# Low parts of eight weight blocks in an encoder's mixer made by an accumulating DMA instead of VectorE

## The chip, the cores and the metric

The kernel runs on one core of one Trainium2 chip. The metric is device time in microseconds (us) of one execution; before the change it is 876.37 us, the median of 3 runs (875.76 to 877.21). Engines are named as in the profile: PE is TensorE (its matmuls; PEld its weight loads), DVE is VectorE, ACT is ScalarE, POOL is GpSimd, SP is SyncE, which issues most DMAs.

## The reference

One encoder layer on 512 positions of 1024 channels: a half-step SwiGLU, a mixer and a second half-step SwiGLU, each behind an RMSNorm, and a final norm. The change is in the mixer:

```python
h = rms_norm(x, mix_norm)
u = h @ w_in                       # 512 Fourier columns | 8 query heads | 2 key heads | 2 value heads
f_out = fourier_mixer(u[..., :o0], fnet_w, fnet_b)     # real part of a 2-D DFT per group, then a 128x128 map per group
a_out = gqa_attention(u[..., o0:o1], u[..., o1:o2], u[..., o2:], q_norm, k_norm)
x = x + jnp.concatenate([f_out, a_out], axis=-1) @ w_out
```

Queries and keys are normed per head and rotated by position; the attention is a plain softmax over all 512 positions.

## The kernel before

**Products in three passes.** All data is float32. A factor is split into a high part, rounded to the type fp32r that PE takes, and a low part, the exact difference. `product` (L108) makes three matmuls: high by high (L109), high by low (L110) and low by high (L111). So each 128x1024 block of weights (`weights`, L95) needs three steps before PE can use it: a load from DRAM into one of three raw buffers (`raw_tile`, L85, on SP's queue), a rounded copy to the high part (L101 on ACT; L99 on DVE for the names in `HI_DVE`, the first two Fourier blocks), and a subtraction on DVE for the low part (`lows`, L72). The third pass alone reads the weights' low part.

**A second way** exists for a few blocks of the first FFN, `rest_by_dma` (L90): ACT writes minus the high part into the low part's place (L92), and a DMA issued by POOL reads the weights from DRAM once more and adds them there (L93). In the kernel before, the four gate blocks with `by_dma` and two activation tiles (L270) take it.

**Slots.** High and low parts live in slots of 128x1024: four of `ring` and two more that the mixer adds (`more`, L610), handed out in turn by `slot` (L77). So three blocks of weights are there at a time, and a block's copy waits until PE has done the block three before it.

**The mixer (L608 to L983).** It multiplies the normed activations by the key block (`in0`), the first query block (`in1`), the values (`in5`) and three further query blocks (`in2` to `in4`), then by four Fourier blocks (`f0` to `f3`, `fload` and `fproject`) and, through `fold`, by the map's weights `fw`, which have half the size. Keys, queries and values pass through `rope`, `query`, `keys` and `value_stacks`, which are work for ACT and DVE. Three tables for the Fourier part (`chan`, `pos`, `odd`, L903) are loaded by POOL at the start.

**Attention and filling.** For 32 pairs of a query tile and a 128-row group, `scores` makes two matmuls on PE, a maximum on DVE (L842) and an exponential on ACT (L845); `turn` transposes the probabilities on PE (L851), copies them rounded on ACT (L854) and subtracts on DVE; `values` makes two matmuls with them (L870, L871). Between these steps the list `fill` spreads the remaining products: query blocks 1 to 3, the eight pieces of the Fourier projection, the fold and the DFT. Each entry has a cost, and entries are taken in order until their sum keeps up with the share of attention steps done (L965 to L972). The blocks' loads are entries of cost 0 in this list (`load`, `fload`).

**What sets the order.** In the FFNs PE and SP keep the order in which the program is written (`in_order`, L64). The mixer stands outside of that: there the order of the instructions on every engine is settled when the program is built, by a model of their times and with earlier lines of the program going first among those that are ready. On the chip each engine then runs its own list strictly in order.

Of the kernel before, what the change touches and what calls it, by code (L numbers as in the profile page):

```python
# [31 lines left out]
PIECES = (0, 2, 2, 1, 1, 1, 1)  # L32
KH = KD // 2
HI_DVE = ("f0", "f1")
SWAP_DMA = ("q1", "q2", "q3")


def asf(ap):
    return ap.bitcast(F32)
# [3 lines left out]
def encoder(ctx, tc, A, out):  # L43
# [27 lines left out]
    def lows(lo, src, hi):  # L71
        nc.vector.tensor_tensor(out=lo, in0=src, in1=asf(hi), op=ALU.subtract)  # L72
# [9 lines left out]
    def weight_slots():  # L82
        return (slot().rearrange("p (a b) -> p a b", b=P) for _ in range(2))

    def raw_tile(src, name, n=KD):  # L85
        raw = wp.tile([P, KD, P], F32, tag="raw", name=f"raw_{name}")
        nc.sync.dma_start(out=raw[:, :n, :], in_=src)
        return raw

    def rest_by_dma(lo, hi, src):  # L90

        nc.scalar.activation(lo, asf(hi), AF.Copy, scale=-1.0)  # L92
        nc.gpsimd.dma_start(out=lo, in_=src, accum_op=ALU.add)  # L93

    def weights(src, name, n=KD, raw=None, by_dma=False):  # L95
        raw = raw or raw_tile(src, name, n)
        hi, lo = weight_slots()
        if name in HI_DVE:
            nc.vector.tensor_copy(hi[:, :n, :], raw[:, :n, :])  # L99
        else:  # L100
            nc.scalar.copy(hi[:, :n, :], raw[:, :n, :])  # L101
        if by_dma:
            rest_by_dma(lo, hi, src)
        else:
            lows(lo[:, :n, :], raw[:, :n, :], hi[:, :n, :])
        return hi, lo
# [6 lines left out]
    class Norm:  # L113
# [36 lines left out]
        def add(self, k):  # L150
            self.scale(k)
            self.sums(k)
# [55 lines left out]
    def ffn(norm, after, wgu, wd, wdt, opening, closing):  # L208
# [6 lines left out]
        with tc.tile_pool(name=f"act{n_}", bufs=1) as ap, tc.tile_pool(name=f"sums{n_}", bufs=2) as sp:  # L215
# [11 lines left out]
            def gate(c, between={}, by_dma=False):  # L227
                whi, wlo = weights(wgu[c], f"gu{n_}_{c}", by_dma=by_dma)
                ps = bank(f"gu{n_}_{c}")
                for k in range(KD):  # L230
                    between.get(k, int)()
                    product(ps, whi[:, k, :], wlo[:, k, :], hh[k], hl[k], k == 0, k == KD - 1)
                return ps
# [169 lines left out]
            def down(d, group, gi):  # L403

                js = [j for j in group if j != "t"]
                whi, wlo = weights(wd[d][:, js[0] : js[-1] + 1, :], f"dn{n_}_{d}_{gi}", len(js))
                w = wt[d // 4][:, d % 4 * P : (d % 4 + 1) * P]

                def steps(ps, t):
                    for i, j in enumerate(group):  # L410
                        h, l = (at[:, where[j], o, t] for o in range(2))
                        first, last = i == 0, i == len(group) - 1
                        if j == "t":
                            nc.tensor.matmul(ps[:, t], w, h, start=first, stop=False)
                            nc.tensor.matmul(ps[:, t], w, l, start=False, stop=last)
                        else:
                            k = j - js[0]
                            product(ps[:, t], whi[:, k, :], wlo[:, k, :], h, l, first, last)
                        yield

                return steps
# [186 lines left out]
    with tc.tile_pool(name="mix", bufs=1) as mp, tc.tile_pool(name="mixt", bufs=1) as mt:  # L608
# [18 lines left out]
        def project(c, name):  # L627

            whi, wlo = weights(A["wins"][c], f"in{c}")
            ps = bank(name)  # L630
            banks[name] = ps

            def step(k):
                product(ps, whi[:, k, :], wlo[:, k, :], hh[k], hl[k], k == 0, k == KD - 1)

            return [(0.65, step, (k,)) for k in range(KD)]
# [3 lines left out]
        def rope(name, g):  # L640
# [4 lines left out]
            sw = tp.tile([P, S], F32, tag="g", name=f"sw_{name}")  # L645
            if name in SWAP_DMA:
                own = mt.tile([P, S], F32, tag="own", name=f"own_{name}")
                nc.scalar.activation(own, ps, AF.Copy, scale=g)
            for b in range(4):
                o, i = b * 32, (b ^ 1) * 32  # L650
                if name in SWAP_DMA:
                    nc.sync.dma_start(out=sw[o : o + 32], in_=own[i : i + 32])
                else:
                    nc.scalar.activation(sw[o : o + 32], ps[i : i + 32], AF.Copy, scale=g[i : i + 32])
            r = tp.tile([P, S], F32, tag="u", name=f"rot_{name}")
            if name in SWAP_DMA:
                nc.vector.tensor_tensor(out=r, in0=own, in1=cos, op=ALU.mult)
# [266 lines left out]
        for t in (1, 2, 3):  # L924
            for k in range(KD):
                add(step, t, k, cost=0.65)
                if k == 0 and t < 3:
                    add(load, t + 1)
                if t == 3 and k in (0, 4):
                    add(fload, k // 4)  # L930
                if k == 3:
                    add(*((value_stacks,) if t == 1 else (heads, f"q{t - 1}", t, scale)), cost=0.3)
            add(query, t)
# [235 lines left out]
```

## Time and profile before

The profiled execution took 877.47 us, 875.7 of them the span of the program, with a mean granted clock of 0.996. From the page and the trace:

| what | value |
|---|---|
| median of runs | 876.37 us (875.76 to 877.21) |
| profiled execution, span | 877.47 us, 875.7 us |
| first matmul of the key block | 351.58 us |
| first matmul of the values, and the first that reads their low part | 364.67 and 365.22 us |
| first matmul of the Fourier blocks | 402.38 us |
| first matmul of the fold | 454.91 us |
| subtraction for a 128x1024 low part (L72, DVE) | 1.22 us |
| rounded copy of 128x1024 (L101, ACT) | 1.05 us |
| such a copy on DVE (L99) | 0.69 us |
| plain load of 512 KB, from issue to landing | 3.4 to 3.8 us at the median, by group |

Busy time says how long an engine had instructions running. A wait is idle time of an engine, put down to the instruction that ended last among those it waited for. What a wait of PE costs is time; what another engine waits for costs nothing unless PE waits for it in turn.

### The profile page before, as it was taken

Reading aid. Unit: us, or ns where it says so; the run is one execution under the profiler, and the core shown is the slowest. Engines: PE = TensorE matmul, PEld = TensorE weight load, DVE = VectorE, ACT = ScalarE, POOL = GpSimd, SP = SyncE. Lnnn points to the kernel's source line nnn. Section 1 sums busy time; section 2 is a strip of 40 time slices with the busy share of each in tenths; the row PEclk is TensorE's granted clock in tenths of the full one; section 3 lists DMA queues with packets and bytes.
Section 4 is the critical chain, followed back from the end, with each engine's and each line's share of the span. In section 5 each row is a group of like instructions: output and inputs, shape, how many; then the busy total and the mean of one; then the engine's idle time right before and its main releaser. Section 6 shows DMA issues by size and latency. Waiting matters only on the chain.

```text
span 875.7 us, 13587 instructions
## 1 busy us (share of the span) xinstructions
PE 862.0 (98%) x5391; PEld 769.1 (88%) x5391; DVE 640.8 (73%) x1011; ACT 459.0 (52%) x763; POOL 27.8 (3%) x33
## 2 busy tenths in 40 slices
PE   8999999999999999999999999999999999999996
PEld 6788998899989998888888888889998999889986
DVE  7798985488746837699888558987974698559554
ACT  7663664266524644677776445535652366226541
POOL 0110000000000000211000000000000000000001
PEclk9999999999999999999999999999999999999999
DMA  7664322323243113621110224242323232323212
GB/s 263 154 150 149 133 85 73 115 97 120 78 140 108 49 51 109 205 79 43 49 49 25 77 70 142 85 133 97 109 79 127 75 117 99 97 101 104 73 37 97
DMA packets 30609, 88.46 MB, mean 101 GB/s; under 512 B 3665, under 2 KB 8529, under 8 KB 30417
## 3 DMA queue, kind: packets, MB, share of 16 engines
q1 hardware_dynamic: 28304, 82.87, 28.3%
q0 software_dynamic: 1696, 4.20, 2.4%
q8 instruction: 42, 0.69, 0.3%
q10 hardware_dynamic: 544, 0.52, 0.2%
q14 instruction: 23, 0.18, 0.1%
HBM read 83.91 MB, written 2.10 MB: 98 GB/s over the span
## 4 chain that ended last, share of the span: by engine, by line
PE 94%; ACT 2%; DVE 2%; DMA 1%; issue 1%; SPq 0%; POOL 0%; DVEq 0%; ACTq 0%
PE r L338 22%; PE q L338 11%; PE dn L109 8%; PE dn L111 8%; PE dn L110 8%; PE p L338 6%; PE gu L109 3%; PE gu L111 3%; PE gu L110 3%; PE out L109 2%; PE out L111 2%; PE out L110 2%; PE pt L851 1%; PE q L109 1%; PE q L110 1%; PE q L111 1%
## 5 line engine op out<-in xcount | busy, mean ns | idle before, releaser
L338 PE MATMUL r<-rt,ring 128*128 128x256 f32 x1632 | 213.0, 282 | 0.0
L338 PEld LDWEIGHTS r<-rt,ring 128*128 128x128 f32 x1632 | 201.8, 188 | 2.4
L109 PE MATMUL dn<-at,ring 128*128 128x512 f32 x303 | 119.7, 395 | 0.0
L110 PE MATMUL dn<-at,ring 128*128 128x512 f32 x303 | 119.6, 395 | 0.0
L111 PE MATMUL dn<-at,ring 128*128 128x512 f32 x303 | 119.6, 395 | 0.0
L338 PE MATMUL q<-rt,ring 128*128 128x256 f32 x816 | 107.9, 281 | 0.0
L424 DVE SCALAR_TENSOR_TENSOR gx<-dn,gx 128x512 f32<-128x512 f32 x61 | 42.1, 690 | 82.0 <-PE dn L111 82.0
L338 PEld LDWEIGHTS q<-rt,ring 128*128 128x128 f32 x816 | 101.6, 188 | 0.0
L72 DVE TENSOR_TENSOR ring<-s,ring 128x1024 fp32r<-128x1024 f32 x68 | 82.9, 1221 | 17.8 <-PE r L338 10.9
L101 ACT CAST ring<-raw_dn 128x768 fp32r<-128x768 f32 (+1 forms) x59 | 45.5, 775 | 92.9 <-PE dn L110 78.8
L299 ACT CAST ring<-s 128x1024 fp32r<-128x1024 f32 x68 | 71.4, 1050 | 38.1 <-PE r L338 18.4
L111 PEld LDWEIGHTS dn<-at,ring 128*128 128x128 f32 x303 | 56.9, 188 | 13.8 <-DVE ring L72 0.2
L110 PEld LDWEIGHTS dn<-at,ring 128*128 128x128 f32 x303 | 57.0, 188 | 13.1
L109 PEld LDWEIGHTS dn<-at,ring 128*128 128x128 f32 x303 | 56.9, 188 | 13.0
L72 DVE TENSOR_TENSOR ring<-raw_dn,ring 128x768 fp32r<-128x768 f32 (+1 forms) x59 | 51.8, 881 | 7.2 <-ACT ring L101 6.2
L72 DVE TENSOR_TENSOR ring<-raw_g,ring 128x1024 fp32r<-128x1024 f32 x34 | 41.6, 1224 | 17.7 <-PE p L338 10.7
L338 PE MATMUL p<-rt,ring 128*128 128x256 f32 x408 | 54.0, 281 | 0.0
L338 PEld LDWEIGHTS p<-rt,ring 128*128 128x128 f32 x408 | 50.8, 188 | 0.0
L299 ACT CAST ring<-raw_g 128x1024 fp32r<-128x1024 f32 x34 | 35.7, 1049 | 22.2 <-DMA raw_g<-in_wgu 9.0
L308 ACT CAST ring<-raw_u 128x512 fp32r<-128x512 f32 x34 | 21.1, 621 | 39.3 <-PE dn L111 19.9
L383 DVE TENSOR_TENSOR u<-g,u 128x512 f32<-128x512 f32 x34 | 23.4, 688 | 15.9 <-ACT u L382 15.9
L109 PE MATMUL gu<-ring 128*128 128x512 f32 x80 | 31.3, 392 | 0.0
(328 smaller groups left out, 1579.9 us busy)
## 6 DMA issues: line engine op xcount, KB each, us to landing
raw_dn<-in_wd SPq DMA_DIRECT2D x48, 384.0 KB, 3.1
raw_g<-in_wgu SPq DMA_DIRECT2D x34, 512.0 KB, 3.8
raw_u<-in_wgu SPq DMA_DIRECT2D x34, 512.0 KB, 4.4
raw_gu<-in_wgu SPq DMA_DIRECT2D x14, 512.0 KB, 3.5
raw_o<-in_wo SPq DMA_DIRECT2D x8, 512.0 KB, 3.6
raw_dn<-in_wd SPq DMA_DIRECT2D x16, 192.0 KB, 2.4
raw_in<-in_wins SPq DMA_DIRECT2D x6, 512.0 KB, 3.6
raw_f<-in_winf SPq DMA_DIRECT2D x4, 512.0 KB, 3.8
```

The source lines that it names most:

```text
L72: nc.vector.tensor_tensor(out=lo, in0=src, in1=asf(hi), op=ALU.subtract)
L101: nc.scalar.copy(hi[:, :n, :], raw[:, :n, :])
L109: nc.tensor.matmul(ps, whi, mhi, start=first, stop=False)
L110: nc.tensor.matmul(ps, whi, mlo, start=False, stop=False)
L111: nc.tensor.matmul(ps, wlo, mhi, start=False, stop=last)
L299: nc.scalar.copy(hi, src)
L308: nc.scalar.copy(hi, src)
L338: nc.tensor.matmul(ps, a[:, ks], b[:, i], start=first and i == 0 and o == 0, stop=i == KH - 1 and o == 2, skip_group_check=not first,)
L383: nc.vector.tensor_tensor(out=u, in0=b["g"], in1=u, op=ALU.mult)
L424: nc.vector.scalar_tensor_tensor(out=x[d][:, t], in0=ps[:, t], scalar=0.5, in1=x[d][:, t], op0=ALU.mult, op1=ALU.add)
L851: nc.tensor.transpose(pt[:, c * P : (c + 1) * P], prob[t, b, c][:, kc * P : (kc + 1) * P], ident)
```

## The change

The names in a new list, `LOW_DMA`, take the second way in `weights`: the values (`in5`), query blocks 1 to 3 (`in2` to `in4`), Fourier blocks 0 to 2 and the map's weights. The key block, the first query block and the last Fourier block keep the subtraction on DVE. `rest_by_dma` gets slices, since the map's weights fill half a tile. And the entry that starts Fourier block 1 in the list `fill` stands behind step 1 of the last query block, not behind step 4.

```diff
 HI_DVE = ("f0", "f1")
+LOW_DMA = ("in5", "in2", "in3", "in4", "f0", "f1", "f2", "fw")
 SWAP_DMA = ("q1", "q2", "q3")
...
-        if by_dma:
-            rest_by_dma(lo, hi, src)
+        if by_dma or name in LOW_DMA:
+            rest_by_dma(lo[:, :n, :], hi[:, :n, :], src)
         else:
             lows(lo[:, :n, :], raw[:, :n, :], hi[:, :n, :])
...
-                if t == 3 and k in (0, 4):
-                    add(fload, k // 4)
+                if t == 3 and k in (0, 1):
+                    add(fload, k)
```

## The prediction

> **What bounds the kernel now.** I read the engine totals first, then the list of what TensorE (PE) waited for in the mixer, then busy times by stage, and last the order of work round each stall. The totals:
>
> ```profile
> PE 862.0 (98%) x5391; PEld 769.1 (88%) x5391; DVE 640.8 (73%) x1011; ACT 459.0 (52%) x763; POOL 27.8 (3%) x33
> ```
>
> PE is busy for 862.0 of 875.7 us: at most 13.7 us can be had from waits, wherever they are. The change touches only the mixer, whose first load is used at 351.58 us and whose last probabilities are used near 478. There PE waited for this (us in total, times, longest):
>
> ```profile
> PE o L870 <- ACT ph L854: 1.4, 2, 0.9
> PE f L761 <- ACT e L845: 1.2, 1, 1.2
> PE s L838 <- ACT e L845: 0.5, 1, 0.5
> PE pt L851 <- ACT e L845: 0.4, 1, 0.4
> ```
>
> The sum is 3.5 us, and that is the ceiling of any gain (0.4%). By the order of time the five stalls are 1.25 us up to 402.38, 0.90 up to 435.83, 0.49 up to 457.03, 0.40 up to 464.71 and 0.48 up to 469.46. The stages, with the columns PE, PEld, DVE, ACT, POOL, granted clock, DMA share, GB/s:
>
> ```profile
> 345.00:370.00 25.00, 25.00 (x120) 20.77 (x120) 16.01 (x25) 14.96 (x21) 5.30 (x5) 1.00 0.53 179
> 370.00:385.00 15.00, 15.00 (x79) 12.57 (x78) 14.45 (x31) 10.08 (x18) 1.64 (x1) 1.00 0.26 83
> 385.00:400.00 15.00, 15.00 (x83) 12.47 (x82) 14.50 (x30) 11.88 (x26) 1.64 (x1) 1.00 0.24 58
> 400.00:415.00 15.00, 13.75 (x99) 12.42 (x98) 13.39 (x33) 11.49 (x24) 3.89 (x3) 1.00 0.11 36
> ...
> 430.00:445.00 15.00, 14.10 (x100) 12.74 (x99) 12.07 (x26) 9.32 (x21) 0.87 (x1) 1.00 0.12 38
> ```
>
> From 370 to 400 VectorE (DVE) is busy 28.95 of 30 us and ScalarE (ACT) 21.96. PE hides that until 401. So DVE is the fuller helper, but every stall of PE ends on an ACT instruction.
>
> **What each sum by DMA costs.** The first FFN already makes low parts this way, and those rows are the price list (ns: min, median, max; the first for the extra copy, the second for the issue and, in us, from issue to landing):
>
> ```profile
> L92 ACT ACTIVATE ring<-ring x3: 1056/1057/1064, 26.3 to 45.0; 128x1024 fp32r<-128x1024 f32 x3
> ```
>
> ```profile
> L93 POOL DMA_DIRECT2D ring<-in_wgu x3: 854/875/1109, 27.6 to 46.3; - x3
> ...
> DMA to landing us min/median/max: 5.2/5.7/7.5
> ```
>
> Removed from DVE: seven subtractions of 128x1024 at 1.22 us (L72, from raw_in and raw_f) and one of 128x512 at 0.68 (raw_fw): 7 x 1.22 + 0.68 = 9.2 us. Added to ACT: seven copies of minus the high part at 1.06 and one of half the size, which I estimate at 0.63 from the 512-wide copies: 8.0 us. Added to GpSimd (POOL): eight issues of some 0.9 us, 7.2 us in all. The low part is then there about 1.06 + 5.7 = 6.8 us after the high part, not 1.2. The weights are also read a second time: in the stretch 20 to 60 us six such sums (2.88 MB) took 42.8% of 40 us of all 16 engines, 3.1 us for each 512 KB, while 3.90 MB of plain loads took 28.8%, 1.5 us for 512 KB.
>
> **Which low part comes late.** For each block I compare the high part's end with the first matmul that needs the low part. Queries: high parts end at 358.1, 365.3 and 371.4. Their extra copies may stand behind the rope and key copies on ACT (free again at 361.4, 369.4, 375.1), so sums are issued by about 362.5, 370.4 and 376.2 and land by 369.5, 376.5 and 382.5; needed at 372.1, 378.3 and 387.8. Fourier blocks: needed from 402.6 (cast 378.1), 404 (cast 386.4) and 428 (cast 394.2), the map's weights (cast 426.0) at 454.9. All these are in time by 2 us or more and cost PE nothing; if the cover of the third block in the list (needed at 378.3) were gone, each us of lateness is a us of PE.
>
> The values' block is the tight one. Its high part runs 352.49 to 353.54, the squares of the closing FFN follow on ACT until 354.7, so I put the extra copy at 354.7 to 355.75 and the issue at 355.8. By then three tables stand ahead of it on POOL's queue:
>
> ```profile
> pos<-in_pos POOLq DMA_DIRECT2D x1, 1028.0 KB, 9.4
> ...
> chan<-in_chan POOLq DMA_DIRECT2D x1, 256.0 KB, 3.9
> ...
> odd<-in_odd POOLq DMA_DIRECT2D x1, 1.0 KB, 9.2
> ```
>
> odd has 1 KB, was issued at 353.17 and took 9.2 us: it came behind pos, so this queue goes in order. pos lands at 352.63 + 9.4 = 362.0. The DMA engines are full (share 0.97 to 1.01 from 358 to 362, 0.28 by 363 to 364). If the sum's data starts at 361 it takes 3.1 us alone and up to 2 more beside what is left of the loads, and some 1 us to be seen: 365 to 367. PE needs it at 365.22, the third matmul of the values. **Cost +1.0 us** (bounds 0 and +2.5). Behind that matmul on PE stand the key transposes, the head sums and the next query block; nothing else can go ahead of them there. Before it, v's first two matmuls run as now.
>
> The Trainium skill's page "DMA: Bandwidth & Descriptors", section "Anatomy of one DMA — SWDGE (gpsimd) path", gives 2.0 us plus bytes over 436 GB/s, an estimate of 3.2 us for 512 KB. The trace has 5.2 to 7.5 us for the accumulating form, so I use the trace; by the page's figure the sum would start with pos gone and be there by about 364, and the total below would be 1.0 us lower. The same page, section "Queues, rings and completion order", says that a ring's descriptors are consumed in order while an engine goes round between the rings, with which odd's 9.2 us agrees.
>
> **What the freed DVE time is worth.** The stall at 402.38 ends with an exponential that ACT starts at 401.43. ACT had run without a gap from 394.18 to 398.94 (the cast of the third Fourier block, then the last query's square, its scaled copy and its casts, a probability cast, an exponential), and then waited for PE's transposes. So there ACT, not DVE, is in front: the third Fourier block's extra 1.06 us may fall just there. On the other hand the exponentials waited 11.2 us in eleven places for DVE's maxima, and DVE loses 4 x 1.22 = 4.9 us of work between 372 and 397. Bounds: the whole stall gone (-1.25), or two extra copies (second and third Fourier block) in front of it (+2.1). I take -0.4, since ACT still has idle time to take the copies, 3.1 us in 384 to 401. The stall at 435.83 goes back to DVE, full from 424.2 to 432.6, with an exponential that waited 3.0 us for it: one subtraction of 0.68 fewer there, and ACT idle to take the map's copy. I take -0.6 (bounds -0.9 and 0). The last three stalls lie among the output weights' casts, which stay as they are: 0, between -1.4 (the order of the engines outside the FFNs is set anew when the program is built) and +1.0 by the same token.
>
> **The moved load.** Three things of that block can move. Its load is already out at 366.61 on SP, right behind the first block's, held by a raw buffer and not by its place; on SP nothing of this stage stands between. Its cast on DVE starts at 386.36, 0.2 us after the second query's last matmul frees the slots (386.16 to 386.55), and a place three steps earlier can't pass that. Its sum is issued at about 388.2 on POOL, ahead of or behind one power of 1.64 us for the heads, and is needed at 404. Cost 0; if the power had to wait for the issue, 0.9 us that the 8 us to the scales' use cover. Raw buffers come free 1.2 us sooner, which only moves loads that wait for nothing.
>
> **Sum.** +1.0 - 0.4 - 0.6 + 0 = 0.0 us on the profiled execution, 877.47 us (875.7 of span and 1.8 around it). It lies 1.1 us above the median of the runs, 876.37, so I forecast 876.4 for the median. About 0.2%, or 1.75 us, is what a measurement can tell from no change.
>
> **Rivals.** (1) DVE is what holds the attention stage back. For it: 28.95 of 30 us busy, and the exponentials' 11.2 us. Against it: every stall ends on ACT, and 402.38's is full of ACT work. Then the first two stalls go (-2.15), and if the new order clears part of the last three (1.37) and the values' sum is in time, -2.2 to -3.5: about 873.5.
>
> (2) ACT takes DVE's place, which makes it slower. Place: 384 to 401, where ACT has 3.1 us idle in pieces of about 0.9 and gets two extra copies of 1.06; a piece too short moves every exponential behind it. Each moved exponential holds its bank and so the scores and the Fourier matmuls. Price 2.1 us there and some 0.5 among the keys (ACT full from 370.3 to 375.1): +2.5, so 878.9. It decides once ACT's idle time in that stretch is under 1 us. Against it: most waits of the exponentials end on DVE.
>
> (3) The values' sum lands at 368, because the copy and its issue come late or the loads of the queries crowd it: PE stands 2.5 to 3 us at 365.22, nothing is won back, 879. For it: full DMA engines and an in-order queue. Against it: by 363 these engines are nearly idle.
>
> **How the numbers follow.** Forecast 0.34, with its own range 874.8 to 878.0; rival 1 0.32; rival 2 0.20; rival 3 0.14. Faster than 874.6: 0.28 of rival 1 and 0.03 of the forecast, 0.31. Slower than 878.1: 0.16 of rival 2, 0.12 of rival 3 and 0.03 of the forecast, 0.31. The rest, 0.38, is within 0.2%. The range 873.2 to 879.6 takes in rivals 1 and 2 and most of 3, and leaves about a tenth on each side.
>
> **What would show it.** The values' third matmul (L111, out v) with an idle time before it, released by a DMA, shows the first term; none shows it 0. The wait of f L761 for the exponential shows the second: gone for rival 1, over 1.25 us for rival 2, with ACT above 16 of 17 us in 384 to 401. The wait before o L870 near 435 shows the third. The forecast is wrong if PE's waits in the mixer add up to less than 1.7 us or over 5.3, or if the new order of the engines moves work between stages so that the stalls can't be paired at all.

## The result, and the profile after

The kernel after takes 878.42 us (median of 22 runs, 876.84 to 881.69), the kernel before in the same session 877.41 us (22 runs, 875.76 to 878.20). The medians lie 1.0 us apart; the ratio worked out from all runs is 1.0017, with a 95% interval from 1.0010 to 1.0024: slower by about 1.5 us. That is inside the 0.2% that counts as no change here, though the interval leaves out 1.

The totals of the profile after and its queue of software-made DMAs (packets, MB, share of 16 engines over the span):

```profile
span 876.7 us, 13601 instructions
PE 861.5 (98%) x5391; PEld 767.9 (88%) x5391; DVE 634.0 (72%) x1003; ACT 466.4 (53%) x771; POOL 34.3 (4%) x41
q0 software_dynamic: 2848, 8.13, 5.1%
```

So the change does what it says: VectorE has eight instructions fewer, ScalarE and POOL eight more each, VectorE down 6.8 us over the span (8.5 between 345 and 480, 114.12 to 105.58), ScalarE up 7.4, POOL up 6.5, and this queue carries 3.93 MB more than the 4.20 MB it carried before. VectorE's relief did not make the kernel faster. What TensorE waited for in the mixer, between 340 and 515 us (us in total, times, longest):

```profile
PE o L871 <- ACT ph L855: 2.5, 3, 1.1
PE pt L852 <- ACT e L846: 0.7, 2, 0.4
PE v L112 <- DMA more<-in_wins: 0.6, 1, 0.6
PE s L839 <- ACT e L846: 0.5, 1, 0.5
PE s L839 <- ACT own_q L649: 0.4, 1, 0.4
```

Line numbers are one higher than before. The sum is 4.7 us for 3.5. The wait at `v` is new. The wait of `f` for an exponential is gone as a line, but three others stand in its place. Placed in time, stall by stall (idle time of TensorE, us; columns worked out from the timelines of the two profiles):

| where | before | after | difference |
|---|---|---|---|
| values' third matmul, 364.1 | 0 | 0.61 | +0.61 |
| 397 to 403, last query block and third Fourier projection | 1.25 | 0.41 + 0.28 + 1.07 = 1.76 | +0.51 |
| 436 | 0.90 | 0.93 | 0 |
| 457, 465, 469.5 | 0.49 + 0.40 + 0.48 | 0.49 + 0.40 + 0.46 | 0 |

A stall costs a little more than its idle time, since the matmuls on both sides of it lose their overlap (one takes about 0.40 us here and the next starts 0.23 us after it): by the distance of their starts the two rows that changed cost 0.77 us (from 0) and 2.41 us (from 1.52), +0.8 and +0.9 us. They make 1.7 of the 1.9 us by which the mixer grew. Its length is taken from the first matmul of the key block to the first of the output projection that stands behind the last matmul of the Fourier part (two pieces of the output projection run a little earlier): 127.02 us before, 128.96 after. I use this length for the experiments, each time from the one execution that was profiled, because the opening of the kernel, which nothing here touches, varies by 2 us between profiles (the mixer starts at 351.6 and 349.7) and blurs the whole time.

The windows that the prediction showed of before, now of after (us, PE, PEld, DVE, ACT, POOL, granted clock, DMA share, GB/s):

```profile
345.00:370.00 25.00, 24.39 (x120) 20.00 (x120) 12.63 (x22) 18.36 (x24) 7.15 (x8) 1.00 0.76 221
370.00:385.00 15.00, 15.00 (x76) 12.52 (x76) 10.93 (x25) 12.22 (x22) 3.48 (x3) 1.00 0.90 192
385.00:400.00 15.00, 14.36 (x75) 11.13 (x74) 13.62 (x31) 11.73 (x23) 4.24 (x3) 1.00 0.44 92
400.00:415.00 15.00, 13.81 (x100) 12.65 (x101) 12.70 (x32) 12.13 (x26) 3.17 (x4) 1.00 0.33 69
```

The clock is 1.00 throughout. VectorE has 10.93 us of work from 370 to 385 where it had 14.45, and the DMA engines are busy for 0.90 of the time where it was 0.26. What became of VectorE's free time is seen in its timeline and in ScalarE's (start, duration, operation, and in brackets the idle time before it and what ended it):

```profile
382.70 0.17 DVE L674 TENSOR_TENSOR sc<-pq_q,r 128x8 f32<-128x8 f32 x1 [0.36 <-PE pq_q L669]
385.40 0.69 DVE L661 TENSOR_TENSOR sw_q<-sw_q,sin 128x512 f32<-128x512 f32 x1 [2.53 <-DMA sw_q<-own_q]
```

```profile
386.85 0.62 ACT L689 CAST qa<-rot_q 64x512 fp32r<-64x512 f32 x1 [3.33 <-DVE rot_q L662]
```

VectorE waits 2.53 us for the four small copies that swap the halves of query block 1 between partitions, and ScalarE, which has the cast of that result next in its order, stands 3.33 us behind it. Before, the same wait was 0.32 us:

```profile
383.81 0.69 DVE L660 TENSOR_TENSOR sw_q<-sw_q,sin 128x512 f32<-128x512 f32 x1 [0.32 <-DMA sw_q<-own_q]
```

The copies themselves landed in 1.9 to 3.1 us before and take up to 5.2 now:

```profile
DMA to landing us min/median/max: 1.9/2.4/5.2
```

VectorE is then busy for 12.93 of the 13.45 us from 385.40 to 398.85, and ScalarE, after another 1.32 us behind it, is bunched. From 395.41 to past 403 it has no gap, and the last of TensorE's three stalls ends on the probability casts at 401.64, which stand behind the extra copy of Fourier block 2 (1.07 us at 399.94):

```profile
396.69 1.05 ACT L102 CAST more<-raw_f 128x1024 fp32r<-128x1024 f32 x1
...
399.17 0.80 ACT L846 ACTIVATE e<-s,mx,sc 128x512 f32<-128x512 f32 x1
...
399.94 1.07 ACT L93 ACTIVATE more<-more 128x1024 fp32r<-128x1024 f32 x1
400.88 0.79 ACT L846 ACTIVATE e<-s,mx,sc 128x512 f32<-128x512 f32 x1
...
401.64 1.58 ACT L855 CAST ph<-pt 128x512 fp32r<-128x512 f32 x3
```

Two places thus need a cause: the values' sum, and the stretch from 383 to 403.

### The profile page after: what moved, and what is told of

Its sections match the earlier page's. It is cut to its first block, busy times and chain, and to the rows that moved or that the text cites. A ratio compares the mean times of both kernels' runs of the same rounds, so it can differ in the third digit from the quotient of the medians.

```text
span 876.7 us, 13601 instructions
## 1 busy us (share of the span) xinstructions
PE 861.5 (98%) x5391; PEld 767.9 (88%) x5391; DVE 634.0 (72%) x1003; ACT 466.4 (53%) x771; POOL 34.3 (4%) x41
## 4 chain that ended last, share of the span: by engine, by line
PE 92%; ACT 3%; DMA 2%; DVE 1%; issue 1%; SPq 0%; POOL 0%; DVEq 0%; ACTq 0%
PE r L339 22%; PE q L339 11%; PE dn L110 8%; PE dn L111 8%; PE dn L112 8%; PE p L339 6%; PE gu L110 3%; PE gu L112 3%; PE gu L111 3%; PE out L110 2%; PE out L112 2%; PE out L111 2%; PE pt L852 1%; DMA more<-in_wins 1%; PE f L762 1%; PE f L763 1%
```

## The experiments

An edit can change more than it says here: outside the feed-forward stages the order of each engine's instructions is set anew when the program is built. Where an experiment left TensorE's and ScalarE's order as it is in the kernel after (*e1*, *e2* but for the one copy that it takes away, *e8*, *e9*, *e10* and *e12*), I say so; those compare cleanly. "Mixer" is the length defined above, "396 to 404" the idle time of TensorE in that stretch.

**The values' sum.** Theory A says that it is late because three tables stand ahead of it in POOL's queue. Its issue and theirs, in the kernel after:

```profile
350.19 0.60 POOL L904 DMA_DIRECT2D chan<-in_chan  x1 [300.93 <-PE dn L112]
350.78 0.58 POOL L904 DMA_DIRECT2D pos<-in_pos  x1
351.33 0.56 POOL L904 DMA_DIRECT2D odd<-in_odd  x1
354.08 0.89 POOL L94 DMA_DIRECT2D more<-in_wins  x1 [2.20 <-ACT more L93]
```

*e1_tables_behind*: the tables are issued behind the sum (same order elsewhere).

```diff
...
-        for t, n in ((chan, "chan"), (pos, "pos"), (odd, "odd")):
-            nc.gpsimd.dma_start(out=t, in_=A[n])
+        with tc.issue_after(sums["in5"].ins):
+            for t, n in ((chan, "chan"), (pos, "pos"), (odd, "odd")):
+                nc.gpsimd.dma_start(out=t, in_=A[n])
```

> The three tables (chan, pos, odd) are issued on POOL's queue behind the sum for the values, not ahead of it; nothing else is edited. Theory A (the values' sum is late because POOL's DMA queue goes in order and 1284 KB of tables stand ahead of it): the sum lands 5.5 to 7 us after its issue at about 354.1, not 10.0, PE's wait at the values' first low matmul (0.61 us in the changed kernel) is gone, and the mixer, from the key block's first matmul to the first of the output weights, takes 128.2 us, not 129.0. Rival (all 16 engines are full then, whatever the order): the sum still takes 9 us or more and PE waits 0.3 us or more. The stalls between 397 and 403 stay at 1.8 us in both.

*e2_no_values*: `"in5"` is taken out of `LOW_DMA` (same order elsewhere).

> The values' block goes back to the subtraction on DVE; the other seven sums stay. Theory A: PE's wait of 0.61 us for the DMA is gone, the stalls between 397 and 403 stay near 1.8 us, the mixer takes 128.2 us, and the time is about 0.8 us under the changed kernel's, ratio to the kernel before 1.0008. Rival (the new order of the engines as a whole costs the time, not this wait): the mixer stays at 128.8 or more.

Measured: no wait for a DMA at the values' third matmul in either. The mixer takes 128.2 us with the tables behind and 128.3 us without the values' sum, for 129.0. TensorE's waits with the tables behind:

```profile
PE o L873 <- ACT ph L857: 2.5, 3, 1.1
PE pt L854 <- ACT e L848: 0.7, 2, 0.4
PE s L841 <- ACT e L848: 0.5, 1, 0.5
PE s L841 <- ACT own_q L651: 0.4, 1, 0.4
PE pt L854 <- DVE sc L676: 0.2, 1, 0.2
```

It is the list of the kernel after with the DMA taken out (the last line, 0.2 us, is new); everything later stays. A holds: with the tables behind it the sum lands 6.68 us after its issue, and its wait, which comes from the tables' place in the queue, costs 0.6 to 0.7 us of the mixer in these two, and more (0.8 to 1.0) in two later runs (*e10* and *e12*) where no wait like that of the last line joins. The whole time does not show it: the ratios are 1.0020 [1.0008, 1.0032] and 1.0012 [1.0003, 1.0021], for 1.0017 with the wait. The wait itself varies from one execution to another: 0.61 us in the kernel after, 0.17 to 0.96 in four other kernels whose values' sum also stands behind the tables (e3, e5, e8 and e9 below).

**Third Fourier block's copies on ScalarE (theory B).** The stall near 402 ends on ScalarE, and this block's cast and extra copy are in front of it.

*e3_no_f2*: `"f2"` is taken out of `LOW_DMA`; its low part is VectorE's again.

> The third Fourier block goes back to the subtraction on DVE; the other seven sums stay. Theory B (between 384 and 402 ACT is in front, and the extra copies of the second and third Fourier block stand before the probabilities' copies there): waits of PE between 397 and 403 fall from 1.8 us to 1.2 or less, and the mixer takes 128.1 us. Rival (the stall there belongs to DVE or to the queries' chain): they stay at 1.6 us or more.

*e5_hold*: both copies are held behind the eleventh exponential; *e7_no_values_hold* the same without the values' sum; *e6_before_hold* the same in the kernel before (there it holds the cast alone, since the subtraction is VectorE's).

```diff
-            h, l = weights(src, f"f{i}", raw=fws.get(i))
+            if i == 2:
+                with tc.issue_after(exps[10].ins):
+                    h, l = weights(src, f"f{i}", raw=fws.get(i))
+            else:
+                h, l = weights(src, f"f{i}", raw=fws.get(i))
...
-            nc.scalar.activation(e, ps, AF.Exp, bias=mx, scale=f, accum_out=zs[t][:, c, b : b + 1])
+            exps.append(nc.scalar.activation(e, ps, AF.Exp, bias=mx, scale=f, accum_out=zs[t][:, c, b : b + 1]))
```

> The changed kernel, but the copies of the third Fourier block on ACT (rounded copy and minus copy) are held behind the eleventh exponential, some 10 us later. Theory B (ACT is in front between 394 and 402, and these two copies of 1.05 us stand there before probabilities): PE's waits between 397 and 403 fall from 1.76 us to 0.7 or less, the mixer takes 127.9 us or less against 129.0. Rival (the last query's chain and latency make the wait): 1.4 us or more stay. PE's wait for the values' sum stays at 0.6 to 1.0 us in both.

> The kernel before, with no sum by DMA in the mixer and no move, but with the third Fourier block's copy on ACT and its subtraction on DVE held behind the eleventh exponential. Theory B: PE's wait of 1.25 us near 402 falls to 0.5 or less and the mixer takes 126.2 us or less against 127.0, ratio 0.999. Rival (DVE or latency makes it): it stays at 1.0 us or more.

> The changed kernel without the values' sum, and with the third Fourier block's copies held as in the run beside it. Theories A and B add up: no wait for a DMA, waits between 397 and 403 of 0.7 us or less, mixer 127.2 us, ratio to the kernel before 1.0000. If the freed DVE time is worth something once ACT is out of the way, 126.5 us or less; if the new order costs time by itself, 128 or more.

| kernel | 396 to 404 | near 435 | mixer | ratio to before |
|---|---|---|---|---|
| before | 1.25 | 0.90 | 127.0 | 1 |
| after | 1.76 | 0.93 | 129.0 | 1.0017 [1.0010, 1.0024] |
| e3_no_f2 | 0.84 + 0.62 = 1.46 | 0.30 | 127.9 | 1.0003 [0.9993, 1.0012] |
| e5_hold | 0.25 + 2.39 = 2.64 | 0.29 | 128.3 | 1.0030 [1.0019, 1.0042] |
| e7_no_values_hold | 0.36 + 2.39 = 2.75 | 0.30 | 128.0 | 1.0027 [1.0017, 1.0036] |
| e6_before_hold | 0.57 | 1.51 | 126.7 | 1.0005 [0.9993, 1.0017] |

B falls in the form in which I put it: it asked for 0.7 us or less with the copies held, and 2.64 and 2.75 us were measured; for *e3_no_f2*, 1.46 us lies between B's 1.2 and the rival's 1.6. With the copies out of the way in *e5_hold* ScalarE waits 1.39 us for VectorE's maxima, then runs two exponentials, and the probability casts start at 402.37 and are late again, by more:

```profile
PE o L875 <- ACT ph L859: 3.1, 3, 2.4
```

In the kernel before the same hold more than halves the stall near 400 and gives the time back near 434. A stall of this stage moves when it is pushed. Without the third block's sum the two places together are 0.9 us better than in the kernel after (1.76 for 2.69), and with seven of the eight sums its time can't be told from before; but the order of the engines is another too, so this doesn't say that the copy alone did it. Its mixer of 127.9 us has a wait of 0.96 us for the values' sum in it; the version without this block's sum and with the tables behind the values' sum was not run.

**Who makes the extra copy.** *e4_neg_pool*: the eight copies of minus the high part go to POOL.

```diff
-    def rest_by_dma(lo, hi, src):
+    def rest_by_dma(lo, hi, src, pool=False):
...
-        nc.scalar.activation(lo, asf(hi), AF.Copy, scale=-1.0)
+        if pool:
+            nc.gpsimd.tensor_scalar(out=lo, in0=asf(hi), scalar1=-1.0, scalar2=None, op0=ALU.mult)
+        else:
+            nc.scalar.activation(lo, asf(hi), AF.Copy, scale=-1.0)
...
-            rest_by_dma(lo[:, :n, :], hi[:, :n, :], src)
+            rest_by_dma(lo[:, :n, :], hi[:, :n, :], src, name in LOW_DMA)
```

> The eight copies of minus the high part are made by POOL instead of ACT; the sums stay. Theory B: with 8.0 us off ACT and 9.2 us off DVE the waits between 397 and 403 fall under 1.0 us and the mixer takes 127.5 us or less beside a wait for the values. Rival (the engines' share of work does not matter, latency does): those waits stay at 1.6 us or more. If POOL takes over 2 us for a copy, the values' sum is issued past 357 and PE's wait there grows to 1.5 us or more, on either theory.

Measured: 882.3 us, ratio 1.0058 [1.0045, 1.0072], mixer 132.1 us. POOL takes 2.77 us for a copy that takes ScalarE 1.06:

```profile
364.38 2.77 POOL L94 TENSOR_SCALAR ring<-ring 128x1024 fp32r<-128x1024 f32 x1
```

The values wait 2.0 us for their sum in place of 0.6, and the longest wait for probability casts is 2.6, just past the stretch that the expectation names. B is not settled by it, since the lateness of POOL's copies is in all of these waits. POOL is no place for these copies.

**The moved load.** *e8_unmoved*: Fourier block 1 is entered at its old place (same order on every engine).

```diff
-                if t == 3 and k in (0, 1):
-                    add(fload, k)
+                if t == 3 and k in (0, 4):
+                    add(fload, k // 4)
```

> The changed kernel, with the second Fourier block's load entry back behind step 4 of the last query block. Theory: the move does nothing by itself, since the slots come free only after the second query's last matmul: the mixer stays at 129.0 within 0.3 us. Rival (the place matters through the order on ACT and POOL): it differs by 0.5 us or more.

Measured: mixer 128.9 us for 129.0, and the same three stalls at 397 to 403 within 0.01 us; the wait for the values' sum is 0.25 us in place of 0.61, and one of 0.40 us for VectorE joins. No instruction changes its place on any engine, so the move does nothing at all. The ratio is 1.0028 [1.0017, 1.0040] where the kernel after, with the same order on every engine, has 1.0017: two such ratios can lie that far apart.

**Why the swap copies land late (theory C).** The sums' own traffic seemed the cause: the DMA engines are busy 0.90 of the time from 370 to 385.

*e9_cut_in3_in4* and *e10_cut_all_but_f0* keep every instruction in its order and cut the named sums to 64 KB each; the rest of those low parts is left at minus the high part. The edit is that of the first; in the second `CUT` names all blocks but f0.

```diff
+CUT = {'in3': 1, 'in4': 1}
...
-    def rest_by_dma(lo, hi, src):
+    def rest_by_dma(lo, hi, src, m=None):
...
-        nc.gpsimd.dma_start(out=lo, in_=src, accum_op=ALU.add)
+        nc.gpsimd.dma_start(
+            out=lo if m is None else lo[:, :m, :], in_=src if m is None else src[:, :m, :], accum_op=ALU.add
+        )
...
-            rest_by_dma(lo[:, :n, :], hi[:, :n, :], src)
+            rest_by_dma(lo[:, :n, :], hi[:, :n, :], src, CUT.get(name, n))
```

> The kernel after, but the sums of in3 and in4 move one of their eight blocks (64 KB in place of 512); the other seven blocks of their low parts stay at minus the high part, so the queries of groups 1 and 2 come out wrong. Every engine's instructions stand in the same order as in the kernel after. Theory C (the sums' traffic delays the swap copies of query group 1, VectorE waits for them at 383, ScalarE stands behind it, and TensorE pays at 397 to 403): the swaps' slowest landing falls from 5.2 us to 3.8 or less, VectorE's wait for sw_q from 2.5 us to 1.3 or less, ScalarE's idle before qa from 3.3 us to 2.2 or less, and TensorE's idle between 396 and 404 from 1.76 us to 1.4 or less; the mixer takes 128.6 us or less for 129.0. Rival D1: the swaps wait for Fourier block 2's plain load and f0's sum, and these numbers stay (wait 2.2 to 2.8). Rival D2: the wait falls, but TensorE's idle there stays at 1.6 to 1.9, because the copies that ScalarE took over and the new order on the engines set it.

> The kernel after, but seven of the eight new sums (all but f0's) move one block of 64 KB each, so their low parts are wrong in the rest (keys' queries, values, Fourier blocks, map); same order of instructions on every engine. What is left of the change is all its work for the engines and none of its traffic but f0's sum. Theory A: the wait at the values' third matmul falls from 0.6 us to 0.2 or less. Theory C: as in the run before for VectorE's wait (1.3 us or less) and TensorE's idle between 396 and 404 (1.4 us or less); with A's part the mixer takes 127.8 us or less. Rival D2: TensorE's idle there stays at 1.6 to 1.9, and the mixer takes 128.0 to 128.4, A's part alone.

*e11_few*: `LOW_DMA = ("in2", "f1", "fw")`, another order on all engines.

> Sums for three blocks alone (in2, f1, fw); values, in3, in4, f0 and f2 have their low parts by VectorE again, as in the kernel before. The engines' orders differ from both kernels. If the loss of the change lies in the values' landing and in the sums that run beside the first swap copies (theories A and C): no wait at the values, VectorE's wait for sw_q 0.5 us or less, TensorE's idle between 396 and 404 at 1.3 us or less, mixer 127.0 within 0.5 us, ratio to before 0.9990 to 1.0005. If sums cost by their copies on ScalarE whichever blocks they serve (rival D2): ratio 1.0005 to 1.0015.

*e12_f3_behind*: in the kernel after, SP has the plain load of Fourier block 3 ahead of the swap copies; before, it stood behind them. It is put behind again, and the tables behind the values' sum, as in the first experiment (same order on TensorE and ScalarE).

```diff
-                fws[i] = raw_tile(src, "f3")
+                with tc.issue_after(swaps["q1"].ins):
+                    fws[i] = raw_tile(src, "f3")
...
```

> The kernel after with two DMAs put elsewhere in their queues and nothing else: on SP the plain load of Fourier block 3 (512 KB) stands behind the four swap copies of query group 1, as in the kernel before, where in the kernel after it stands ahead of them; on POOL the three tables stand behind the values' sum, as in an earlier run. TensorE's and ScalarE's instructions stand in the same order as in the kernel after. Theory E (the sums no longer read the raw tiles, a raw tile comes free sooner, Fourier block 3's load gets ahead of the swap copies and they land behind it): VectorE's wait for sw_q falls from 2.5 us to 0.6 or less, ScalarE's idle before qa from 3.3 us to 1.5 or less, and TensorE's idle between 396 and 404 from 1.76 us to 1.3 or less; the mixer takes 127.7 us or less, the ratio to before is 0.9995 to 1.0010. Rival F: f0's sum, which runs beside the swaps, is what delays them, and the wait stays at 1.8 us or more. Rival D2: the wait falls, but TensorE's idle there stays at 1.6 to 1.95, since ScalarE's copies and the new order set it; the mixer takes 128.0 to 128.4 us and the ratio is 1.0010 to 1.0025, as with the tables moved alone.

| kernel | VectorE's wait for sw_q, query group 1 | ScalarE's idle before its qa | 396 to 404 | mixer | ratio to before |
|---|---|---|---|---|---|
| after | 2.53 | 3.33 | 1.76 | 129.0 | 1.0017 [1.0010, 1.0024] |
| e9_cut_in3_in4 | 2.78 | 3.57 | 0.30 + 1.76 = 2.06 | 128.8 | 1.0016 [1.0007, 1.0024] |
| e10_cut_all_but_f0 | 2.45 | 3.25 | 1.76 | 128.0 | 1.0017 [1.0009, 1.0026] |
| e12_f3_behind | 2.52 | 3.31 | 1.78 | 128.1 | 1.0021 [1.0010, 1.0032] |
| e11_few | 0.32 (group 2: 3.13) | none | 2.87 | 130.0 | 1.0029 [1.0018, 1.0041] |
| before | 0.32 | none | 1.25 | 127.0 | 1 |

C and E both fall. With seven of the eight sums cut the wait is the same, and so is each stall from 397 on; what goes is the values' wait (A's part, 1.0 us of the mixer). TensorE's waits in that kernel:

```profile
PE o L874 <- ACT ph L858: 2.5, 3, 1.1
PE pt L855 <- ACT e L849: 0.7, 2, 0.4
PE s L842 <- ACT e L849: 0.5, 1, 0.5
PE s L842 <- ACT own_q L652: 0.4, 1, 0.4
```

With the load of Fourier block 3 behind the swaps, the wait stays too. The first three swap copies do gain by it: they land in 2.0 us, where they took 4.3 to 4.7 with the load ahead (*e1_tables_behind*, the same kernel but for this load). VectorE waits for the fourth, and that one takes 5.24. SP's and VectorE's lines:

```profile
377.27 2.48 SPq L655 DMA_DIRECT2D sw_q<-own_q  x4
379.85 0.54 SPq L90 DMA_DIRECT2D raw_f<-in_winf  x1
```

```profile
384.52 0.69 DVE L663 TENSOR_TENSOR sw_q<-sw_q,sin 128x512 f32<-128x512 f32 x1 [2.52 <-DMA sw_q<-own_q]
```

What all kernels with this wait have in common is f0's sum, 512 KB that POOL issues 1.2 to 2.4 us after the first of these swaps and before the last of them has landed. In the window 376 to 386 of the kernel with all other sums cut it is the only one on its queue, and its packets hold a third of 16 engines for 10 us, 3.3 us of all of them:

```profile
q0 software_dynamic: 144, 0.52, 32.7%
q1 hardware_dynamic: 336, 0.79, 25.3%
```

The wait at query group 1 is 2.4 to 2.9 us in the eleven kernels that have f0's sum there and 0.3 in the three that haven't (before, e6_before_hold, e11_few). That alone would be no proof, since the order of the engines is another in these three. The packets go further. In *e12_f3_behind* POOL issues f0's sum at 378.49, and SP the four swap copies at 377.27, 377.90, 378.53 and 379.16. From 380.1 to 383.1 the two queues moved this (a share can come out a little over 100%):

```profile
q0 software_dynamic: 123, 0.50, 105.0%
q1 hardware_dynamic: 15, 0.00, 0.4%
```

The sum holds all 16 engines, and the fourth copy's packets move only from 383.13 on. It lands at 384.39, the sum at 384.09; in *e10_cut_all_but_f0* the two land at 383.98 and 384.10. And it need not be f0's sum. In *e11_few*, which has none, POOL issues f1's sum at 389.41, beside the swap copies of query group 2. The last of them, issued at 390.22, lands at 395.31, the sum at 395.14, and VectorE waits for that copy (the profile writes "issue", but it landed 0.08 us before the start):

```profile
395.39 0.69 DVE L661 TENSOR_TENSOR sw_q<-sw_q,sin 128x512 f32<-128x512 f32 x1 [3.13 <-issue]
```

In the kernel after, f1's sum is issued 0.37 us behind the last copy of that group, and these copies land in 1.9 to 2.0 us. So for VectorE's wait rival F holds: a copy that comes up while a sum's packets are moving stands until they are through. (e4_neg_pool is an exception: f0's sum is issued 0.48 us behind the last of the four copies there, and a plain load and an earlier sum are in flight beside them.)

What this wait is worth on TensorE is not settled. Two things speak for a share. The two kernels without any late swap copy, before and e6_before_hold, have 1.25 and 0.57 us in 396 to 404, and all others have more (e4_neg_pool has 0.40 there and 2.65 just behind). And in e11_few and e3_no_f2 the chain that the profile follows back from a stall of this stretch runs through a late copy; in the kernel after it goes through ScalarE's work from 396.05 on and then through TensorE itself.

Rival D2, ScalarE's copies and the new order, is not excluded and not shown either. With the kernel after's order on TensorE and ScalarE, the three stalls of this stretch are 0.41 to 0.42, 0.27 to 0.28 and 1.07 to 1.08 us in all seven kernels (in four of them a wait of 0.16 to 0.40 us for VectorE joins). But VectorE's wait for the late copy is in all seven too, 2.45 to 2.86 us, so none of them tests D2 against F. Against the copies' half of D2 stand e5_hold and e7_no_values_hold, where the stall grew with two of the copies out of the way, though in another order. What is left open is how the 0.5 us of idle time more than before split between ScalarE's extra copies in that stretch, the new order and the wait for the late copy; no kernel here changes one of them alone. The run that would tell was not made: the kernel after with f0's sum issued behind these swap copies. There is room for it, since that sum landed at 386.12 and TensorE's first Fourier matmul is at 402.63.

No version is shown to be faster than the kernel before. The nearest are e6_before_hold, 1.0005 [0.9993, 1.0017], and e3_no_f2, 1.0003 [0.9993, 1.0012].

## Why the prediction was right, and where it was not

The forecast was no change, 876.4 us; 878.42 was measured, 0.2% more, inside the range though above the forecast's own 874.8 to 878.0. By the medians half of this gap is the session (the kernel before took 877.41 us there, 876.37 when the forecast was made), half the change. That it held owes more to the small size of everything in play than to its sum: of the three terms that were not 0 one came true, and the sum of 0.0 us stands against 1.9 us by which the mixer grew. TensorE's waits in the mixer add up to 4.7 us, inside the 1.7 to 5.3 that it allowed itself.

**The ceiling.** Right: VectorE is the fuller helper, and each of TensorE's five stalls in the kernel before ends on ScalarE. Some 8 us less work for VectorE in this stage made nothing faster, and rival 1, by which it would have given 2 to 3.5 us, did not come true. That the other seven sums would be in time came true too (in one case by 1.8 us in the prediction's own numbers, 376.5 for 378.3, not by the 2 it names): no wait of TensorE ends on them.

**The values' sum, +1.0.** Right in mechanism and nearly in size: +0.8 by the distance of the starts, and the first experiment takes it away by the queue's order alone. The sum was issued at 354.08 and landed 10.0 us later, 4.0 us after pos. On this term the trace sided against the page's figure in the prediction: by the formula of the Trainium skill's "DMA: Bandwidth & Descriptors", section "Anatomy of one DMA — SWDGE (gpsimd) path", the estimate was 3.2 us once the tables are gone, and no wait. A wait was measured, and with the tables behind it the same sum took 6.68 and 6.24 us (e1_tables_behind and e12_f3_behind).

**The stall at 402.38, -0.4.** Wrong in sign: +0.9 by the distance of the starts (+0.5 idle), within its bounds of -1.25 and +2.1. The step that failed reads "ACT still has idle time to take the copies, 3.1 us in 384 to 401". ScalarE had that time, but not where it was needed: in the kernel after it stands 3.33 us at 383.5 to 386.85 behind VectorE, and is full from 395.41 on, where the extra copy of the third Fourier block falls. That looks like rival 2, ScalarE in VectorE's place, at a third of its price of 2.5 us, but with the block's copies held the stall grew, so the runs do not show that these copies make it; the late swap copy stands ahead of it as well. The signs that the prediction gave would have misled: ScalarE above 16 of 17 us in 384 to 401 does not show (12.73 us, since the idle part lies in front), and the wait of f for the exponential is gone, which was to mean rival 1.

**The step left out.** For every sum the prediction asked when it lands itself, and never what else is in flight. The swap copies, up to 5.2 us for 3.1, are the transfer that suffered, and VectorE's wait of 2.53 us is what it brought; its price on TensorE is the open part above.

**The stall at 435.83, -0.6.** Wrong: 0.93 for 0.90. One subtraction of 0.68 us fewer on VectorE did not reach TensorE. In five kernels with another order (e3, e4, e5, e7, e11) the same stall is 0.29 or 0.30, with the map's sum in all of them, so it goes with the order of the engines and not with the subtraction.

**The last three stalls and the moved load, 0.** Right: 0.49, 0.40 and 0.46 us for 0.49, 0.40 and 0.48, and the unmoved kernel's mixer is the same to 0.1 us.

## What to carry to other kernels

Work taken off the fullest helper engine is worth nothing until it stands in the chain that ends the main engine's waits; look first at which engine ends each wait, and count what the replacement adds to that one. A DMA queue that goes in order charges an urgent transfer with everything issued before it: put urgent transfers ahead of large ones that nobody needs soon. Look across the queues too: here a small copy on one queue stood behind a large sum on another. When orders are set by the build, compare kernels whose order is the same, by the length of the stage and not by the whole time, before a fraction of a per cent is given a cause. And when a suspect is present in every run that is compared, the runs do not clear it.

## What the runs showed of the hardware that was not expected

- Small copies between partitions (64 KB each) took up to 5.1 to 5.6 us to land in the twelve kernels with sums by DMA in this stage, and at most 3.1 and 2.9 in the two without. The late one came up while a 512 KB sum on another queue was moving: for 3 us the sum had 105.0% of the 16 engines and the copy's queue 0.4%. A plain 512 KB load ahead of the copies on their own queue made 4.3 to 4.7 us of 2.0 for the first three.
- A sum of 512 KB by DMA landed 10.0 us after its issue behind 1,285 KB of tables in its queue; the first feed-forward stage had 5.2 to 7.5.
- POOL takes 2.77 us at the median for a scaled copy of 128 x 1024 that takes ScalarE 1.06.
